# A decoder layer in fp32 on one core: the MLP's first two steps chunk by chunk, and sums and norm products on VectorE

## The chip, the core and the metric

The kernel runs on one core of one Trainium2 chip. The metric is the device time of one launch in microseconds (us). The engines are TensorE (PE in the profile; its weight loads are PEld), VectorE (DVE), ScalarE (ACT), GpSimd (POOL) and SyncE (SP), which here only issues DMAs. POOL issues DMAs too.

## The reference

One inference step of a one-layer decoder: 2048 prompt tokens, and a sample of 8 sequences with 4 new tokens each, which brings its own state. All in fp32, model width 1024.

```python
def rms_norm(x, g):
    y = x * lax.rsqrt(jnp.mean(x * x, axis=-1, keepdims=True) + EPS)
    return y * g

def decoder_layer(x, p, lp, state):          # x: (B, T, 1024)
    xn = rms_norm(x, lp['norm_mix_pre'])
    qk_raw, v_m, o_m, gates, q_a, k_a, v_a = split_projection(xn @ lp['w_in'])
    ...
    # mLSTM heads (y_m) and sliding-window attention heads (y_a)
    ...
    mix = jnp.concatenate([y_m, y_a], axis=-1) @ lp['w_out']
    x = x + rms_norm(mix, lp['norm_mix_post'])
    u = rms_norm(x, lp['norm_ffn_pre'])
    f = jnp.square(jax.nn.relu(u @ lp['w_up'])) @ lp['w_down']      # 1024 -> 4096 -> 1024
    x = x + rms_norm(f, lp['norm_ffn_post'])
    x = x + jax.nn.sigmoid(x @ lp['w_pgate']) * (p @ lp['w_pproj'])
    return x, (c_new, n_new, m_new, conv_new, k_new, v_new)
```

The change touches the MLP (`f`), the norm products around it, and the place in time of the sample's own mLSTM and attention ("decode").

## The kernel before, in words

**Blocks, chunks, groups.** The prompt is 16 blocks of 128 tokens in six chunks (3, 3, 3, 3, 2, 2 blocks). Projection, mLSTM and attention come first, up to about 700 us. The rest runs over three groups of two chunks each (`ci` 0 and 1): the product with w_out (tiles `mo`), the residual and the norms, the MLP, the gate (`pg`, `pv`). Beside the MLP's start runs what the previous stage left over, as side work. The sample's 32 rows travel with the third group, 16 of them in each chunk's columns (`HS`), so that a chunk there has 2 x 128 + 16 = 272 columns; in the first two groups it has 384.

**Products.** Every fp32 product is three fp32r matmuls: each operand is a high part (suffix h) and a low part (suffix l), and high x high, high x low and low x high are added in PSUM (`mm3`, L145 in the profile). To split a value, ACT casts it to the high part and DVE subtracts (L228 and L229: `hh`, `hl`).

**Weights.** `Ring` holds seven tiles `w` of 512 KB (high and low part of a weight block) and five raw buffers. The first use of a weight loads it raw (`wr`) on SP's queue, casts it on ACT (L249), and subtracts on POOL and DVE by turns (L250). If the plan names it again later, the tile is also stored to DRAM (`wk<-w`, L275, POOL's queue, two tiles later). Later uses load the stored pair (`w<-wk`, L282, SP's queue). The generator `plan()` lists all uses in order, and `take(n)` hands out the next n tiles; so the order of loads is the order of the plan.

**Order on PE.** PE's instructions stand in the order in which the code issues them. `Flow` keeps a model of PE's time; at each `pe.tick()` side work whose modelled time has come is put in: transposes of the next chunk's input (`tsp`), and `decode()` for the sample (`dec`; tiles with names that begin with d). `DECW` is the modelled time after which decode starts, counted from the place where it is added. `pe.drain(side)` puts in whatever is left of a side at once. The other engines' instructions are ordered by the tile framework's scheduler.

**The MLP** (`mlp`, from L1590). The 4096 hidden columns are taken in 16 steps of 256 (two tiles of 128, `ft`). Step 0 and step 1 are plain: for each chunk an up product with four weight tiles (`up`, tiles `up`, L1595), then `hidden` (L1612: relu on ACT L1617, square on ACT L1618, split L228 and L229), then the down product with four weight tiles (`down`, tiles `dn`, two for each half of the 1024 output columns), which ACT copies into `f` in step 0 and DVE adds to `f` later (L1728). In the third group chunk 1's down product is transposed (`dn200t` and so on), so that the sample's 32 rows can be taken together; for that POOL copies chunk 0's 16 hidden columns into chunk 1's tile (L1624).

Steps 2 to 15 make the up product for both chunks at once with seven products instead of eight (`up_both`). They need sums and differences of the two chunks' input blocks, made while steps 0 and 1 run: `sums()` makes seven for each half q of the columns (L1641 to L1653, tiles `ts`), each then split into `t0`, `t1`, `t2` (ACT L1658, DVE L1659). In the second and third group the half q = 1 is made on POOL, the rest on DVE. `last_sum()` (L1663 to L1675) overwrites the block that only plain steps need, so it stands behind the last plain up product.

Before the change the order was: step 0, chunk 0 up and down; drain `tsp`; chunk 1 up (with the same four tiles) and down (its four tiles loaded again); step 1: drain `dec`, add the sums; up of chunk 0, up of chunk 1, drain, last sum; down of chunk 0, down of chunk 1. These take 4 + 4 + 4 + 4 + 4 = 20 weight tiles.

**Norm products.** `finished(b, half, g, scale)` (L1433) runs when one half (512 columns) of a block's `mo` or `f` is complete: ACT squares and sums it (`j`, L1441), and the half is multiplied by the norm's gain (`gpost` behind w_out, `gffn` behind the MLP; L1443), on POOL for the first half and on DVE for the second.

Of the kernel before, what the change touches and what calls it, by code (L numbers as in the profile page):

```python
# [9 lines left out]
F32 = mybir.dt.float32  # L10
# [44 lines left out]
UENG = "d", "d", "ppp", "ppp", "", "p", "pp"  # L55
FAST = 2, 2, 2
TSP = 1.4
WBUF = 5
WIDE = 4
DECW = 5.0  # L60
DECF = 1.0
# [134 lines left out]
def hybrid_layer(ctx: ExitStack, tc: tile.TileContext, A, O):  # L196
# [195 lines left out]
    def plan():  # L392
# [36 lines left out]
        for gi in range(len(GROUPS)):  # L429
            for ci in range(2):  # L430
                for half in range(2):
                    for k in range(4):
                        yield row(w_out, k, half)
                    for k in range(4):
                        yield heads(k, half)
            for s in range(STEPS):
                if s >= FAST[gi]:
                    for i in range(7):
                        yield product(s, i)
                else:  # L440
                    for q in pairs:
                        yield two(s, q)
                for half in (0, 1, 0, 1) if s == 0 else (0, 1):
                    for k in range(s * FS, (s + 1) * FS):
                        yield row(w_down, k, half)
            for ci in range(2):
                for half in range(2):
                    embed = 0 if half == 0 and ci == 0 else 4
                    for k in range(KT):
                        if k == embed:  # L450
                            for e in range(2):
                                yield row(w_pp, e, half)
                        yield row(w_pg, k, half)
# [980 lines left out]
    def finished(b, half, g, scale):  # L1434
# [6 lines left out]
        act.activation(junk[:n, :512], v, AF.Square, scale=scale, accum_out=ms[b][:n, half : half + 1])  # L1441
        eng = (pool, dve)[half]
        eng.tensor_tensor(v, v, g[:n, half * 512 : half * 512 + 512], ALU.mult)  # L1443

# [144 lines left out]
    def mlp(gi, chunks, sample):  # L1589
# [24 lines left out]
        def hidden(s, ci, ft, t, src, hid):  # L1614
# [5 lines left out]
            split(*(y[:, :W] for y in hid[ci, ft]), t)  # L1620
            if sample and ci == 1:

                for y, z in zip(hid[0, ft], hid[1, ft]):
                    pool.tensor_copy(z[:, W : W + HS], y[:, W - HS : W].bitcast(F32))  # L1624

# [3 lines left out]
        def sums():  # L1629
# [6 lines left out]
            for q in range(2):  # L1636
                c = slice(q * n, (q + 1) * n)
                (b11, b21), (b12, b22) = [[[y[:, :, c].bitcast(F32) for y in b] for b in B[ci]] for ci in range(2)]
                t1, t2, t4 = [temp(f"ts{i}{q}", n) for i in range(3)]
                eng = pool if q and gi > 0 else dve  # L1640
                eng.tensor_tensor(t1, b12[0], b11[0], ALU.subtract)  # L1641
# [65 lines left out]
        def accumulate(s, ci, names, w, x, out, hid):  # L1707
# [9 lines left out]

            ahead = 3 if s == 0 else 1
            for i0 in range(0, len(names), ahead):
# [32 lines left out]

        X = None
        for s in range(STEPS):
            hid = {}
            fast = s >= FAST[gi]
            if not fast:
                wu = ring.take(4)
            if s == 0:

                up(s, 0, wu, hid)
                for half in range(2):
                    down(s, 0, half, down_weights(), hid)
                pe.drain(tsp)
                up(s, 1, wu, hid)
                for half in range(2):
                    down(s, 1, half, down_weights(), hid)
                continue
            if s == FAST[gi] - 1:
                pe.drain(dec)  # L1770
# [4 lines left out]
                tsp.add(sums())  # L1775
            if fast:
                up_both(s, X, hid)
            else:
                up(s, 0, wu, hid)
                up(s, 1, wu, hid)  # L1780
                if s == FAST[gi] - 1:
                    pe.drain(tsp)
                    last_sum()
            if s == STEPS - 1:
# [194 lines left out]
```

## Time and profile before

| what | value |
| --- | --- |
| runs | 2673.46, 2678.0, 2678.6 us, median 2678.0 |
| the profiled execution | 2676.5 us, of which 2674.7 are the span of the trace |
| mean granted clock of PE | 0.981 |
| DVE busy | 1481.7 us, 55% of the span |
| DMA moved | 632.23 MB, mean 236 GB/s |

In a row of the profile "L1728 DVE TENSOR_TENSOR f<-f,dn" is the instruction from line 1728 on DVE, output before the arrow, inputs behind it, with buffer numbers left out; x420 is how many there are, then the busy time of all in us and the mean of one in ns, then the engine's idle time just before them and what ended most of it. A row of waits names the waiting engine, tile and line, what it waited for, the total in us, the number of times and the longest. A row of the table by stretch gives start and end in us, the length, busy time and count of each engine, the granted clock of PE (1.00 is full speed), and DMA's share and rate. A row of the timeline gives start, duration, instruction, and in brackets the idle time before it with its releaser.

### The profile page before, as it was taken

What the parts mean: (1) busy time and instruction counts of PE and PEld (TensorE: products, weight loads), DVE (VectorE), ACT (ScalarE), POOL (GpSimd) and SP (SyncE); (2) the same over time, 40 slices, a digit from 0 to 9 for tenths busy, and PEclk for the clock granted to TensorE, in tenths of its full rate; (3) what the DMA queues carried; (4) which work ended last, traced back from release to release, by engine and by line L of the source; (5) the groups of instructions that cost most, each with busy time, mean ns of one, the idle gap of its engine ahead of it and who ended that gap; (6) DMA issues with size and microseconds to landing.
All of it is one profiled execution on the core that took longest, in us unless ns stands there. A gap on an engine that the chain in (4) does not pass through costs nothing.

```text
span 2674.7 us, 39114 instructions
## 1 busy us (share of the span) xinstructions
PE 2549.5 (95%) x14260; PEld 2212.9 (83%) x14260; DVE 1481.7 (55%) x3112; ACT 975.9 (36%) x2165; POOL 658.0 (25%) x936
## 2 busy tenths in 40 slices
PE   7899999998899999999998999999999998999998
PEld 6787878877688888888776789988888877999986
DVE  6675666664677655655735564444446345444443
ACT  5545344543455433444513432222223133222231
POOL 5311111111436666666513320000001012000010
PEclk9999999999999999999998999999999998999999
DMA  8765656666786666666987645555557885777786
GB/s 305 268 215 173 217 167 221 210 241 224 255 326 240 254 245 236 236 236 233 341 323 238 209 142 188 189 189 174 173 182 256 288 316 187 254 261 258 257 297 230
DMA packets 215186, 632.23 MB, mean 236 GB/s; under 512 B 24790, under 2 KB 58794, under 8 KB 214977
## 3 DMA queue, kind: packets, MB, share of 16 engines
q1 hardware_dynamic: 169552, 472.19, 52.0%
q0 software_dynamic: 45392, 157.50, 15.1%
q8 instruction: 113, 1.85, 0.3%
q14 instruction: 81, 0.66, 0.1%
q10 hardware_dynamic: 48, 0.03, 0.0%
HBM read 475.47 MB, written 155.25 MB: 236 GB/s over the span
## 4 chain that ended last, share of the span: by engine, by line
PE 74%; DVE 10%; DMA 6%; issue 4%; POOL 3%; ACT 2%; SPq 0%; POOLq 0%; DVEq 0%; ACTq 0%
PE dn L145 20%; PE up L145 20%; PE pg L145 5%; PE mo L145 5%; PE v L145 3%; DMA wk<-w 3%; PE qk L145 2%; DVE hl L229 2%; DMA w<-wk 2%; PE o L145 2%; PE gv L145 2%; PE qa L145 1%; PE aT L149 1%; PE aO L145 1%; PE pv L145 1%
## 5 line engine op out<-in xcount | busy, mean ns | idle before, releaser
L145 PE MATMUL dn<-w,hh 128*128 128x512 f32 x1792 | 566.6, 397 | 13.7 <-DVE f L1449 5.1
L145 PEld LDWEIGHTS dn<-w,hh 128*128 128x128 f32 x1792 | 333.2, 189 | 95.1 <-DVE f L1728 8.6
L1728 DVE TENSOR_TENSOR f<-f,dn 128x512 f32<-128x512 f32 x420 | 286.9, 687 | 222.0 <-PE dn L145 220.9
L145 PE MATMUL dn<-w,hl 128*128 128x512 f32 x896 | 355.5, 397 | 2.5 <-DVE hl L229 2.4
L1692 DVE TENSOR_TENSOR re<-up,re 128x384 f32<-128x384 f32 (+1 forms) x294 | 152.0, 517 | 326.4 <-PE up L145 326.4
L145 PEld LDWEIGHTS dn<-w,hl 128*128 128x128 f32 x896 | 169.0, 189 | 46.3 <-DVE hl L229 7.5
L1693 ACT COPY re<-up 128x384 f32<-128x384 f32 (+1 forms) x42 | 18.9, 450 | 414.8 <-PE up L145 414.8
L1617 ACT ACTIVATE re<-re 128x384 f32<-128x384 f32 (+1 forms) x168 | 83.2, 495 | 207.9 <-DVE re L1692 205.8
L229 DVE TENSOR_TENSOR hl<-re,hh 128x384 fp32r<-128x384 f32 (+1 forms) x192 | 137.7, 717 | 31.1 <-ACT hh L228 30.4
L275 POOL DMA_DIRECT2D wk<-w x242 | 134.0, 555 | 32.2 <-DVE w L250 29.2
L1443 POOL TENSOR_TENSOR f<-f,gffn 128x512 f32<-128x512 f32 x16 | 21.8, 1365 | 476.5 <-ACT j L1441 476.2
L250 POOL TENSOR_TENSOR w<-wr,w 128x512 fp32r<-128x512 f32 (+2 forms) x76 | 104.9, 1380 | 87.5 <-ACT w L249 86.6
L249 ACT CAST w<-wb 128x512 fp32r<-128x512 f32 x98 | 60.7, 621 | 173.2 <-PE dn L145 118.3
L249 ACT CAST w<-wr 128x512 fp32r<-128x512 f32 (+2 forms) x152 | 89.3, 598 | 85.6 <-PE up L145 34.3
L250 POOL TENSOR_TENSOR w<-wb,w 128x512 fp32r<-128x512 f32 x70 | 91.9, 1313 | 116.3 <-ACT w L249 115.8
L1618 ACT ACTIVATE re<-re 128x384 f32<-128x384 f32 (+1 forms) x192 | 95.1, 495 | 5.9
L228 ACT CAST hh<-re 128x384 fp32r<-128x384 f32 (+1 forms) x192 | 92.8, 483 | 6.8
L1043 ACT ACTIVATE s<-s,swt 128x257 f32<-128x257 f32 (+1 forms) x128 | 63.4, 497 | 77.5 <-DVE swt L1040 76.4
L1037 DVE CUSTOM_DVE_ANT_0 s<-aS,cst,sink 128x256 f32<-128x256 f32 (+1 forms) x128 | 57.0, 473 | 59.4 <-PE aS L145 59.2
L1624 POOL CAST hh<-hh 128x16 fp32r<-128x16 f32 x32 | 8.0, 249 | 319.0 <-ACT hh L228 319.0
L145 PE MATMUL up<-t0h,w 128*128 128x384 f32 (+1 forms) x336 | 85.1, 320 | 0.0
L145 PE MATMUL up<-t1h,w 128*128 128x384 f32 (+1 forms) x336 | 85.1, 320 | 0.0
(1537 smaller groups left out, 6530.7 us busy)
## 6 DMA issues: line engine op xcount, KB each, us to landing
w<-wk SPq DMA_DIRECT2D x692, 512.0 KB, 4.7
wk<-w POOLq DMA_DIRECT2D x238, 512.0 KB, 6.6
wr<-in_w_down_dram SPq DMA_DIRECT2D x64, 256.0 KB, 7.7
wb<-in_w_up_dram SPq DMA_DIRECT2D x28, 512.0 KB, 6.8
w<-wk SPq DMA_DIRECT2D x20, 528.0 KB, 4.4
x<-in_x_prompt_dram SPq DMA_DIRECT2D x16, 512.0 KB, 5.2
y<-yd SPq DMA_DIRECT2D x32, 256.0 KB, 7.1
xr<-in_x_prompt_dram SPq DMA_DIRECT2D x16, 512.0 KB, 6.3
```

The costliest lines, as they stand in the source:

```text
L145: ins = self.pe.matmul(out, lhsT, rhs, start=start, stop=stop)
L228: act.copy(hi, src)
L229: dve.tensor_tensor(lo, src, hi.bitcast(F32), ALU.subtract)
L249: act.copy(hi, src)
L250: (eng or weng()).tensor_tensor(lo, src, hi.bitcast(F32), ALU.subtract)
L275: here(put(self.kept[key], t.bitcast(U32)))
L1037: dve.tensor_tensor_reduce(s_[:, s, lo : 2 * P], pS[:, s, lo:], bias[:, j, lo:], 1.0 if s == 0 else 0.0625, sink[:, h : h + 1], ALU.add, A ...
L1043: act.activation(e_, e_, AF.Exp, bias=nm[:, s : s + 1], accum_out=sm[:, s : s + 1])
L1617: act.activation(t, src, AF.Relu)
L1618: act.square(t, t)
L1692: add = lambda out, a, b: dve.tensor_tensor(out, a, b, ALU.add)
L1728: dve.tensor_tensor(out(i), out(i), ps[i], ALU.add)
```

## The change

**Order.** Steps 0 and 1 go chunk by chunk: chunk 0 takes step 0 (up, down) and step 1 (up, down); then `tsp` and `dec` are drained and the sums are added; then chunk 1 takes step 0 and step 1 in the same way, `tsp` is drained and the last sum made. The plan names the weight tiles of both steps once for each chunk, 2 x (4 + 4 + 4 + 4) = 32 tiles. The down product in step 1 now keeps three PSUM tiles open as step 0 did (`ahead`).

**Decode's start.** `DECW` is 12.0 instead of 5.0.

**Norm products.** Both halves are multiplied on DVE.

**Sums.** All sums of the input blocks are made on DVE.

**The sample's columns.** Chunk 0's 16 hidden columns are kept in small tiles (`hs`) for as long as chunk 1 needs them; that is a second small copy on POOL for each of them.

```diff
@@ -53,11 +53,11 @@
 MPACE = 3.0
 GBUF = 2
 UENG = "d", "d", "ppp", "ppp", "", "p", "pp"
-FAST = 2, 2, 2
+FAST = 2
 TSP = 1.4
 WBUF = 5
 WIDE = 4
-DECW = 5.0
+DECW = 12.0
 DECF = 1.0
 UPW = 7.0, 7.0
 UPS = 2.8, 3.5
@@ -433,14 +433,14 @@
                         yield row(w_out, k, half)
                     for k in range(4):
                         yield heads(k, half)
-            for s in range(STEPS):
-                if s >= FAST[gi]:
+            for s in (*range(FAST), *range(STEPS)):
+                if s >= FAST:
                     for i in range(7):
                         yield product(s, i)
                 else:
                     for q in pairs:
                         yield two(s, q)
-                for half in (0, 1, 0, 1) if s == 0 else (0, 1):
+                for half in (0, 1):
                     for k in range(s * FS, (s + 1) * FS):
                         yield row(w_down, k, half)
             for ci in range(2):
@@ -1439,8 +1439,7 @@
         v = f[b][:n, half * 512 : half * 512 + 512]
         junk = jp.tile([P, D], BF16, tag="j", name=f"j{nm}{half}", bufs=2)
         act.activation(junk[:n, :512], v, AF.Square, scale=scale, accum_out=ms[b][:n, half : half + 1])
-        eng = (pool, dve)[half]
-        eng.tensor_tensor(v, v, g[:n, half * 512 : half * 512 + 512], ALU.mult)
+        dve.tensor_tensor(v, v, g[:n, half * 512 : half * 512 + 512], ALU.mult)
 
     def residual(b, rs, x):
         n, nm = tok(b)
@@ -1618,10 +1617,14 @@
             act.square(t, t)
             hid[ci, ft] = [hp.tile([P, UW], F32R, tag=f"h{e}", name=f"h{e}{nm}") for e in "hl"]
             split(*(y[:, :W] for y in hid[ci, ft]), t)
-            if sample and ci == 1:
-
-                for y, z in zip(hid[0, ft], hid[1, ft]):
-                    pool.tensor_copy(z[:, W : W + HS], y[:, W - HS : W].bitcast(F32))
+            if sample:
+
+                for e, y in enumerate(hid[ci, ft]):
+                    if ci == 0:
+                        t = hid["s", ft, e] = small.tile([P, HS], F32, tag="hs", name=f"hs{e}{nm}", bufs=8)
+                        pool.tensor_copy(t, y[:, W - HS : W].bitcast(F32))
+                    else:
+                        pool.tensor_copy(y[:, W : W + HS], hid["s", ft, e])
 
         def temp(nm, n):
             return ring.wide.tile([P, KT // 2, 2 * P], F32, tag="w", name=f"{nm}{G}")[:, :, :n]
@@ -1637,7 +1640,7 @@
                 c = slice(q * n, (q + 1) * n)
                 (b11, b21), (b12, b22) = [[[y[:, :, c].bitcast(F32) for y in b] for b in B[ci]] for ci in range(2)]
                 t1, t2, t4 = [temp(f"ts{i}{q}", n) for i in range(3)]
-                eng = pool if q and gi > 0 else dve
+                eng = dve
                 eng.tensor_tensor(t1, b12[0], b11[0], ALU.subtract)
                 yield TSP
                 eng.tensor_tensor(t4, b12[1], b11[1], ALU.subtract)
@@ -1715,7 +1718,7 @@
                 pe.tick()
 
 
-            ahead = 3 if s == 0 else 1
+            ahead = 3 if s < FAST else 1
             for i0 in range(0, len(names), ahead):
                 part = range(i0, min(i0 + ahead, len(names)))
                 for ft in range(FS):
@@ -1750,37 +1753,28 @@
         def down_weights():
             return [[t[:, :512] for t in w] for w in ring.take(FS)]
 
-        X = None
-        for s in range(STEPS):
-            hid = {}
-            fast = s >= FAST[gi]
-            if not fast:
-                wu = ring.take(4)
-            if s == 0:
-
-                up(s, 0, wu, hid)
-                for half in range(2):
-                    down(s, 0, half, down_weights(), hid)
+        X, hids = None, []
+
+        for ci in range(2):
+            if ci == 1:
                 pe.drain(tsp)
-                up(s, 1, wu, hid)
-                for half in range(2):
-                    down(s, 1, half, down_weights(), hid)
-                continue
-            if s == FAST[gi] - 1:
                 pe.drain(dec)
                 es_lp.close()
                 es_t = ExitStack()
                 tp = es_t.enter_context(tc.tile_pool(name="tp", bufs=1, side="right", reuse_waits="tile"))
                 ring.wide = es_t.enter_context(tc.tile_pool(name="wide", bufs=WIDE, side="right", reuse_waits="tile"))
                 tsp.add(sums())
-            if fast:
-                up_both(s, X, hid)
-            else:
-                up(s, 0, wu, hid)
-                up(s, 1, wu, hid)
-                if s == FAST[gi] - 1:
-                    pe.drain(tsp)
-                    last_sum()
+            for s in range(FAST):
+                if ci == 0:
+                    hids.append({})
+                up(s, ci, ring.take(4), hids[s])
+                for half in range(2):
+                    down(s, ci, half, down_weights(), hids[s])
+        pe.drain(tsp)
+        last_sum()
+        for s in range(FAST, STEPS):
+            hid = {}
+            up_both(s, X, hid)
             if s == STEPS - 1:
                 es_t.close()
                 open_lp()
```

Line numbers move by a few: the sums stand at L1644 to L1656, their splits at L1661 and L1662, the additions to `f` at L1731, the norm product at L1442.

**PE, third group, behind chunk 0's down product of step 0.** `dn` are down products of chunk 0; `ut150t`, `ut151t` and `ut1st` are transposes of the last block and of the sample's rows; `ut20` and `ut21` are the inputs of chunk 0 and chunk 1. Before:

```order
L145 MATMUL dn_20812<-w_20806,hh_20762 128x512 x2
L145 MATMUL dn_20812<-w_20806,hl_20763 128x512
L149 MATMUL ut150t<-ident,f_20408 128x128 x4
L149 MATMUL ut151t<-ident,f_20408 128x128 x4
L149 MATMUL ut1st<-ident,fs 128x32 x8
L145 MATMUL up_20859<-ut21h_20678,w_20666 128x272
```

After:

```order
L145 MATMUL dn_20868<-w_20862,hh_20814 128x512 x2
L145 MATMUL dn_20868<-w_20862,hl_20815 128x512
L149 MATMUL ut150t<-ident,f_20456 128x128 x4
L149 MATMUL ut151t<-ident,f_20456 128x128 x4
L145 MATMUL up_20906<-ut20h_20466,w_20898 128x272
L145 MATMUL up_20906<-ut20l_20468,w_20898 128x272
...
L149 MATMUL ut1st<-ident,fs 128x32 x8
L145 MATMUL up_20959<-ut20h_20466,w_20898 128x272
```

Before, chunk 1's up product stands right behind the transposes of its own last block; after, step 1 of chunk 0 stands there, whose input has been there since before step 0.

**PE, second group, decode's first transposes.** `mo` is the product with w_out in the second group's mix, `dph` the transposes of the sample's convolution rows (`hrow`, loaded from DRAM) and of its projection; `yt9t` to `yt11t` are transposes for chunk 1's mix. Counted from the first `mo` of this stage, 27 `mo` matmuls stand ahead of the first `dph` before, and 54 `mo` matmuls and 12 transposes after. Before:

```order
L145 MATMUL mo_14221<-w_14258,yt10h_13904 128x512 x2
L145 MATMUL mo_14221<-w_14258,yt10l_13906 128x512
L149 MATMUL dph<-ident,hrow 128x24
L149 MATMUL dph<-ident,zqk 128x32
...
L145 MATMUL mo_14221<-w_14260,yt10h_13904 128x512 x2
L145 MATMUL mo_14221<-w_14260,yt10l_13906 128x512
L149 MATMUL yt9t<-ident,y_14234 128x128 x4
```

After:

```order
L149 MATMUL yt11t<-ident,y_14264 128x128 x4
L145 MATMUL mo_14333<-w_14338,yt10h_13929 128x512 x2
L145 MATMUL mo_14333<-w_14338,yt10l_13931 128x512
...
L145 MATMUL mo_14335<-w_14338,yt10h_13929 128x512 x2
L145 MATMUL mo_14335<-w_14338,yt10l_13931 128x512
L149 MATMUL dph<-ident,hrow 128x24
L149 MATMUL dph<-ident,zqk 128x32
```

Decode's first instructions on PE move behind 27 more `mo` matmuls and behind the transposes of three more blocks.

**POOL and DVE, second group, the sums of the half q = 1.** `ts` are the sums, `ut10` and `ut11` the inputs of the two chunks. Before, on POOL:

```order
L1641 TENSOR_TENSOR ts_15762<-ut11h_15133,ut10h_14649 128x4x192
L1643 TENSOR_TENSOR ts_15764<-ut11l_15135,ut10l_14651 128x4x192
L1645 TENSOR_TENSOR ts_15762<-ts_15762,ts_15764 128x4x192
L1647 TENSOR_TENSOR ts_15763<-ut11h_15134,ts_15762 128x4x192
L1649 TENSOR_TENSOR ts_15763<-ts_15763,ut11l_15136 128x4x192
```

After, on DVE, where all fourteen now stand, from the first:

```order
L1644 TENSOR_TENSOR ts_15664<-ut11h_15157,ut10h_14624 128x4x192
L1646 TENSOR_TENSOR ts_15666<-ut11l_15159,ut10l_14626 128x4x192
L229 TENSOR_TENSOR hl_15695<-re_15691,hh_15694 128x384
L1648 TENSOR_TENSOR ts_15664<-ts_15664,ts_15666 128x4x192
L1650 TENSOR_TENSOR ts_15665<-ut11h_15158,ts_15664 128x4x192
L1662 TENSOR_TENSOR t0l_15659<-ts_15664,t0h_15658 128x4x192
L1652 TENSOR_TENSOR ts_15665<-ts_15665,ut11l_15160 128x4x192
L229 TENSOR_TENSOR hl_15730<-re_15726,hh_15729 128x384
```

POOL holds none of the sums any more; on DVE they stand among the splits (L229) of chunk 1's hidden tiles.

## The prediction

> **What bounds it now.** I read the page first: its busy times say that the matrix engine sets the time.
>
> ```profile
> PE 2549.5 (95%) x14260; PEld 2212.9 (83%) x14260; DVE 1481.7 (55%) x3112; ACT 975.9 (36%) x2165; POOL 658.0 (25%) x936
> ```
>
> PE lacks 125 us of the 2674.7 us span, and the edit removes no product. So the question is which waits of PE and which stretches at a reduced clock lie where the edit moves work. I cut the places out with a table by stretch. Its columns are length, then busy time and count for PE, weight loads, DVE, ACT, POOL; granted clock, DMA share, GB/s.
>
> ```profile
> 738.70:776.00 37.30, 37.23 (x176) 30.08 (x175) 21.91 (x45) 17.96 (x37) 14.80 (x19) 1.00 0.92 345
> 775.00:851.00 76.00, 71.96 (x364) 63.10 (x363) 64.01 (x90) 42.16 (x77) 32.63 (x33) 1.00 0.67 235
> 1404.00:1421.00 17.00, 7.97 (x34) 5.95 (x32) 6.52 (x24) 2.31 (x5) 10.75 (x22) 0.60 0.51 149
> 1506.00:1558.00 52.00, 52.00 (x286) 42.36 (x286) 25.94 (x62) 30.97 (x69) 6.71 (x9) 1.00 0.56 190
> 1558.00:1600.00 42.00, 36.94 (x174) 31.88 (x174) 36.11 (x35) 13.00 (x22) 14.41 (x7) 0.96 0.30 100
> 2197.00:2245.00 48.00, 33.05 (x183) 29.39 (x182) 32.69 (x51) 18.53 (x40) 16.47 (x15) 0.79 0.52 179
> 2205.00:2213.00 8.00, 4.15 (x12) 3.29 (x13) 4.01 (x11) 2.61 (x6) 1.89 (x4) 0.57 1.03 396
> 2222.00:2230.00 8.00, 6.63 (x30) 6.43 (x31) 7.93 (x9) 2.01 (x5) 5.05 (x3) 0.57 0.00 1
> 2236.00:2244.00 8.00, 4.17 (x18) 3.97 (x19) 5.52 (x9) 2.77 (x7) 2.27 (x2) 0.57 0.20 80
> 2245.00:2271.00 26.00, 26.00 (x185) 24.93 (x185) 8.97 (x17) 7.80 (x18) 1.33 (x4) 1.00 0.55 190
> ```
>
> Steps 0 and 1 of the first group run from 775 to 851, those of the second from 1506 to 1600, those of the third from 2197 to 2271. The loss grows from group to group. In the third, 183 matmul rows take 48.0 us and the next 185 of about the same mix take 26.0 us, so some 22 us are lost there. The second group loses 5.1 us of idle time and a little clock, the first about 4 us. At 1404 decode's start leaves PE idle for 9 of 17 us.
>
> **What the change does to each.** *First group, 775 to 851.* PE's waits there are these:
>
> ```profile
> PE dn L145 <- DVE hl L229: 1.9, 1, 1.9
> PE dn L145 <- ACT hh L228: 1.0, 1, 1.0
> PE up L145 <- DVE ut01l L237: 0.9, 1, 0.9
> ```
>
> The up product of chunk 1 no longer follows right on its norm (0.9 goes); the turn from hidden to down remains in every step (1.9 and 1.0 may stay: there are four such turns now, three before). What is new are the weights. Before, two steps took 20 tiles; now 32, which is 12 more of 512 KB in each of three groups, 36 loads and 18.9 MB in all.
>
> ```profile
> w<-wk SPq DMA_DIRECT2D x692, 512.0 KB, 4.7
> wk<-w POOLq DMA_DIRECT2D x238, 512.0 KB, 6.6
> ```
>
> Here chunk 0 meets 16 tiles for the first time, one after the other: each is loaded raw (0.26 MB), split, and stored (0.52 MB), 12.6 MB within chunk 0's two steps. Half of the 72 us that PE works between 775 and 851 is 36 us, so 350 GB/s are needed. Row 738.70 is the nearest: there 16 tiles were made at 345 GB/s with PE busy for 37.23 of 37.30 us. 12.6 MB at 345 take 36.5 us. From below, the extra loads hide wholly and the waits go: −4. From above, each of the 12 extra loads shows for 1 us: +12. I take +3, close to the row that kept PE busy. ACT's casts for the next tiles stand ahead of ACT's copies out of PSUM, and a cast waits for the store of the tile whose buffer it takes (6.6 us): that is what the upper end holds.
>
> *Decode's start.* PE comes to decode's first transposes long before their operand has landed, then runs at half clock (0.60 in row 1404.00; a pair of mo matmuls takes 1.22 us instead of 0.62):
>
> ```profile
> 1403.96 0.40 PE L145 MATMUL mo<-w,yt10l 128*128 128x512 f32 x1
> 1413.38 0.27 PE L149 MATMUL dph<-ident,hrow 24*128 24x24 f32 x1 [9.03 <-DMA hrow<-in_state_mlstm_conv_dram]
> 1414.34 1.22 PE L145 MATMUL mo<-w,yt10h 128*128 128x512 f32 x2
> ...
> PE dph L149 <- DMA hrow<-in_state_mlstm_conv_dram: 9.0, 1, 9.0
> PE dpU L145 <- DVE skm L1275: 2.4, 1, 2.4
> PE dpX L145 <- issue: 2.3, 1, 2.3
> PE dn L145 <- ACT hh L228: 2.3, 1, 2.3
> PE dn L145 <- ACT re L1617: 2.3, 1, 2.3
> ```
>
> With DECW at 12, PE's order puts 27 more mo matmuls and 12 transposes ahead of them. At 0.23 us (half a pair's start-to-start) and about 0.1 that is 6.2 + 1.2 = 7.4 us, so PE arrives at about 1411.8 for a landing at 1413.3: about 7.5 of the 9.0 go. The load itself waits for nothing that the edit moves. The half clock behind it ran for some 7 us and lost about 3.5; with a gap of 1.5 I take that as gone. Decode's later steps lie nearer to each other (dpU behind one skm buffer, dpX): between nothing and another 4 us more, I take +1. Sum −10, from −15 to −4.
>
> *Second group's steps.* Of the last two rows both waits of 2.3 us (steps' turns, while half the sums run on POOL and DVE together) have this cause:
>
> ```profile
> L1643 POOL TENSOR_TENSOR ts<-ut11l,ut10l 128x768 f32<-128x768 f32 x1 | 2.5, 2505 | 2.8 <-DVE t0l L1659 2.8
> L1651 DVE TENSOR_TENSOR ts<-ut10h,ts 128x768 f32<-128x768 f32 x1 | 2.5, 2494 | 0.0
> L1647 DVE TENSOR_TENSOR ts<-ut11h,ts 128x768 f32<-128x768 f32 x1 | 1.0, 961 | 0.0
> ```
>
> A DVE sum takes 0.96 us by itself and 2.5 beside POOL's. Now POOL has none: fourteen sums of 0.96 are 13.4 us of DVE, in the about 34 us of PE work of chunk 1's two steps. The 4.6 us of waits and the 1.7 that a clock of 0.96 over 42 us costs go. New are one or two sums queued on DVE ahead of a hidden tile's low half (0 to 1.9) and the last of decode, drained without a product beside it (about 1): net −5, from −9 to +2.
>
> *Third group's steps.* Waits there:
>
> ```profile
> PE dn L145 <- DVE f L1449: 5.1, 1, 5.1
> PE dn200t L145 <- issue: 4.1, 1, 4.1
> PE up L145 <- ACT ut21h L236: 2.3, 1, 2.3
> PE up L145 <- DVE ut21l L237: 1.4, 1, 1.4
> PE dn200t L145 <- ACT re L1617: 1.2, 1, 1.2
> ...
> 2234.16 1.70 POOL L1651 TENSOR_TENSOR ts<-ut20h,ts 128x544 f32<-128x544 f32 x1
> 2235.81 0.69 POOL L1624 CAST hl<-hl 128x16 fp32r<-128x16 f32 x1
> 2236.46 1.81 POOL L1653 TENSOR_TENSOR ts<-ut20l,ts 128x544 f32<-128x544 f32 x1
> ```
>
> The 5.1 stay: that residual waits for a load which SyncE issues behind the gain's load, and neither is moved. The 2.3 and 1.4 go, since step 1 of chunk 0 now stands between chunk 0's down product and chunk 1's up product. The 1.2 and the 4.1 come while the sample's little copies stand on POOL between sums of 1.7 us; both reasons leave POOL. That is 9.0. The clock was 0.57 in three places (rows 2205, 2222, 2236); the first follows the 5.1 and stays, the other two have 4 to 7 us of work at half rate each, say 5.5 lost together. New: sums queued ahead of the hidden tiles' splits, about 2 as above; and 32 tiles, 16.8 MB, in the about 48 us of PE work there, 350 GB/s, for which row 2205 shows 396 and row 738.70 shows 345: about 0.5 more. Net −12, from −18 (nothing new) to −4 (5 us of weight waits, one clock dip staying).
>
> *The norm's products.*
>
> ```profile
> L1443 POOL TENSOR_TENSOR f<-f,gffn 128x512 f32<-128x512 f32 x16 | 21.8, 1365 | 476.5 <-ACT j L1441 476.2
> L1443 DVE TENSOR_TENSOR f<-f,gffn 128x512 f32<-128x512 f32 x16 | 13.0, 812 | 4.2 <-ACT j L1441 4.1
> ```
>
> Thirty-two products of 1.37 us on POOL become some 0.8 on DVE. Each belongs to the first half of a block, and the second half's comes later, so it isn't last in the chain; DVE, busy for 55%, takes 26 us more in pieces between PE's matmuls. Zero, from −2 to +4.
>
> Sum: +3 − 10 − 5 − 12 + 0 = −24. Against the profiled execution's own 2676.5 that is 2652.5; the median of the runs, 2678.0, lies 1.5 above it, so **2654**.
>
> [...] Row 2222 has a clock of 0.57 with PE busy for 6.63 of its 8 us, and the only waits ahead of it are the 2.3 and 1.4: here gaps that short already cost clock. [...]
>
> **Rivals.** *The clock doesn't come back.* If the dips of row 2222 and of the second group come from something other than the short gaps, their 2.7 and 1.7 stay: −20, 2658. [...] Chance 0.07.
>
> *The stalls only move.* DVE now holds everything that POOL did, and chunk 1's hidden tiles queue behind sums at all eight places of groups two and three: 1.9 each is 15, which eats those groups' gain to −2; with decode's −10 and +3 to +5 elsewhere that leaves −8, 2670. For it: hl waits already appear among PE's. Against: DVE was free for 16 of 48 us in row 2197 with its operations stretched by POOL. Chance 0.16.
>
> *Weights become the bound (slower).* Place: chunk 0's 16 made tiles in the first group, and all 32 in the third, where down and up leave about 1.5 us a tile. It decides by the rate reached: together 29.4 MB must pass beside 80 us of PE work without loss, at 370 GB/s. If only the 235 of row 775 are reached, these take 125 us, 45 more, and the second group's 16.8 MB take 71 instead of 67, 4 more. All else at its best gives −39 (decode −15, second group −9, third −9 of waits and −5.5 of clock); so +10, 2688. The break-even is at about 250 GB/s. For it: the stores and casts wait on each other, and DMA showed 235 in just this stage. Against: that stage asked for no more, and 345 and 396 stand in the rows. Chance 0.17.
>
> *All waits go* and nothing new comes, each term at its lower end: −4 − 15 − 9 − 18 = −46, 2632. Chance 0.08.
>
> **How the numbers follow.** The forecast keeps 0.52. Its terms' spreads, added as squares (8, 6, 6, 7, 3), give about 14 us either side, 2640 to 2668. The range for 8 in 10 reaches to 2636 below (half of the last rival outside) and to 2676 above, which takes in the moved stalls and leaves out the slower rival. A measurement of this kernel can tell about 0.2%, 5.4 us, from no change. Faster by more: nearly all of 0.52, 0.07, 0.10 of the moved stalls, 0.08: 0.76. Within: 0.04 of the moved stalls, 0.03 of the slow case, 0.01: 0.08. Slower: 0.16.
>
> **What would show it.** In the changed profile: the wait for hrow near 1.5 us and the stretch behind it at full clock; no wait of PE on chunk 1's ut in the third group's steps, no 4.1 us gap there, but the 5.1 again; DVE sums of 0.96 us throughout; in the first group a DMA share near 0.9 in chunk 0's steps with PE still busy for over 90%. Wrong: PE waits on "w" of several us in steps 0 and 1 (the slower rival), or many hl waits of 1 to 2 us (moved stalls).

## The result, and the profile after

Four runs of the changed kernel took 2653.0 to 2659.81 us, median 2657.02, beside 2675.73 for the kernel before: a ratio of 0.9934, 95% interval 0.9919 to 0.9949. Six later runs of it had a median of 2651.17 and a ratio of 0.9917, 0.9901 to 0.9933. So it is faster by 19 to 23 us; 24 were forecast, from 2678.0, the median of its first three runs, to 2654. Executions of one kernel spread widely: the one before had 2666 to 2681 in all comparisons, so single stages are compared below rather than totals.

The page of the changed kernel, the line of the engines:

```profile
PE 2545.7 (96%) x14260; PEld 2211.4 (83%) x14260; DVE 1480.7 (56%) x3160; ACT 974.4 (37%) x2165; POOL 596.6 (22%) x952
```

The span fell from 2674.7 to 2655.4, PE's busy time hardly: what went is waiting. Now the stages between the same landmarks, in rows of the table by stretch (start and end, length; PE, weight loads, DVE, ACT, POOL; clock, DMA share, GB/s). Before: first group's steps 0 and 1 (to the first sum product of step 2), second group's mix (from its first `mo` to its first `up`), second group's steps, third group's steps.

```profile
775.60:855.20 79.60, 75.56 (x385) 66.78 (x385) 64.10 (x90) 43.51 (x80) 36.79 (x38) 1.00 0.65 230
1397.90:1506.50 108.60, 94.83 (x446) 72.19 (x445) 54.51 (x145) 32.66 (x74) 43.12 (x69) 0.91 0.75 237
1506.50:1603.70 97.20, 92.14 (x478) 77.54 (x477) 61.90 (x95) 44.14 (x91) 21.12 (x15) 0.98 0.46 155
2197.60:2273.80 76.20, 61.25 (x385) 56.65 (x384) 41.89 (x68) 26.38 (x59) 17.80 (x19) 0.87 0.55 188
```

After, in the same order:

```profile
773.00:863.30 90.30, 80.09 (x386) 70.18 (x385) 65.66 (x90) 42.74 (x80) 30.67 (x38) 0.92 0.77 273
1406.90:1510.60 103.70, 96.67 (x447) 72.90 (x446) 54.77 (x151) 33.22 (x74) 32.20 (x59) 0.92 0.79 245
1510.60:1601.40 90.80, 90.08 (x478) 76.58 (x477) 56.23 (x102) 44.32 (x91) 7.07 (x13) 1.00 0.70 239
2191.30:2256.40 65.10, 58.28 (x386) 53.16 (x385) 39.20 (x75) 25.93 (x59) 8.45 (x20) 0.95 0.87 319
```

The first group lost 10.7 us, its clock fell to 0.92; the other three stages gained 4.9, 6.4 and 11.1. That is 11.7 gained in all. The remaining 7.6 of the 19.3 lie in many places: 2.2 ahead of 701 us, in code that the edit doesn't touch, 4.0 between the second group's steps and the third's, and 1.9 behind the third group's steps.

PE's waits after, the longest of each place: first group (two rows), second group's mix and steps (five), third group's steps (two).

```profile
PE dn L145 <- DVE hl L229: 6.5, 3, 3.8
PE dn L145 <- ACT hh L228: 3.7, 2, 2.1
...
PE dpU L145 <- DVE skm L1275: 2.4, 2, 1.6
PE mo L145 <- DMA w<-wk: 1.8, 1, 1.8
PE dpI L145 <- DVE sW L1208: 1.5, 1, 1.5
PE dph L149 <- DMA hrow<-in_state_mlstm_conv_dram: 0.8, 1, 0.8
PE dn L145 <- ACT hh L228: 0.5, 1, 0.5
...
PE dn L145 <- ACT ju L1480: 4.5, 1, 4.5
PE dn200t L145 <- DVE hl L229: 0.6, 1, 0.6
```

As forecast, hrow's wait is nearly gone, the 5.1 of the third group stays (4.5, now put down to the operation behind that residual), and the waits for chunk 1's input and the 4.1 have gone. Not forecast: 10.2 us of waits for hidden tiles in the first group, and two new waits of 1.8 and 1.5 in the mix, where the 2.3 for `dpX` have gone.

The longest of the first group's waits, in the timelines of DVE, POOL and PE (start, duration, instruction, idle time before it):

```profile
785.45 2.39 DVE L250 TENSOR_TENSOR w<-wr,w 128x512 fp32r<-128x512 f32 x1
787.76 2.40 DVE L237 TENSOR_TENSOR ut01l<-g,ut01h 128x512 fp32r<-128x512 f32 x1
790.08 0.55 DVE L229 TENSOR_TENSOR hl<-re,hh 128x384 fp32r<-128x384 f32 x1
...
785.99 1.29 POOL L250 TENSOR_TENSOR w<-wr,w 128x512 fp32r<-128x512 f32 x1
788.32 1.27 POOL L250 TENSOR_TENSOR w<-wr,w 128x512 fp32r<-128x512 f32 x1
...
790.68 0.79 PE L145 MATMUL dn<-w,hl 128*128 128x512 f32 x1 [3.81 <-DVE hl L229]
```

PE waits for `hl`. It takes DVE 0.55 us, but stands behind two operations of 2.4 us, and each of these runs beside a subtraction of POOL for a weight tile. The same DVE operation (L237) takes 0.68 at 784.79, where POOL only issues stores. This turn from hidden to down costs PE 5.4 of the 10.2 us (1.5 for `hh` and 3.8 for `hl`). The other waits lie at two later turns, 2.7 and 2.2 us:

```profile
810.76 0.83 ACT L1661 CAST t2h<-ts 128x768 fp32r<-128x768 f32 x1 [1.57 <-DVE ts L1656]
811.50 0.52 ACT L1617 ACTIVATE re<-re 128x384 f32<-128x384 f32 x1
...
849.54 2.07 DVE L229 TENSOR_TENSOR hl<-re,hh 128x384 fp32r<-128x384 f32 x1
849.91 1.27 POOL L307 TENSOR_TENSOR wb<-wb 128x512 f32<-128x512 f32 x1
```

At the first of them ACT casts a sum, for which it waits for DVE, ahead of the hidden tile's square. At the second the split itself takes 2.07 beside a POOL operation that prepares weights for step 2; the kernel before has an `hl` wait of 1.9 in this stage too, at another turn.

### The profile page after: what moved, and what is told of

It reads as the page before. It is cut to its first block, busy times and chain, and to the rows that moved or that the text cites. A ratio compares the mean times of both kernels' runs of the same rounds, so it can differ in the third digit from the quotient of the medians.

```text
span 2655.4 us, 39328 instructions
## 1 busy us (share of the span) xinstructions
PE 2545.7 (96%) x14260; PEld 2211.4 (83%) x14260; DVE 1480.7 (56%) x3160; ACT 974.4 (37%) x2165; POOL 596.6 (22%) x952
## 4 chain that ended last, share of the span: by engine, by line
PE 74%; DVE 10%; issue 6%; DMA 5%; ACT 3%; POOL 2%; SPq 0%; DVEq 0%; POOLq 0%; ACTq 0%
PE up L145 22%; PE dn L145 21%; PE mo L145 5%; PE pg L145 4%; PE v L145 3%; PE qk L145 2%; DMA w<-wk 2%; PE qa L145 2%; PE gv L145 2%; DVE hl L229 2%; PE o L145 1%; DMA wk<-w 1%; PE aT L149 1%; PE aO L145 1%; PE pv L145 1%
## 5 line engine op out<-in xcount | busy, mean ns | idle before, releaser
L145 PE MATMUL dn<-w,hh 128*128 128x512 f32 x1792 | 567.4, 398 | 11.7 <-ACT hh L228 4.6
L1731 DVE TENSOR_TENSOR f<-f,dn 128x512 f32<-128x512 f32 x420 | 287.1, 686 | 209.7 <-PE dn L145 207.5
L229 DVE TENSOR_TENSOR hl<-re,hh 128x384 fp32r<-128x384 f32 (+1 forms) x192 | 135.3, 705 | 44.9 <-ACT hh L228 43.9
L1454 POOL TENSOR_TENSOR ms<-ms,nhalf 128x1 f32<-128x1 f32 x32 | 19.8, 629 | 587.5 <-DVE ms L1453 569.0
L249 ACT CAST w<-wb 128x512 fp32r<-128x512 f32 x98 | 60.4, 620 | 169.9 <-PE dn L145 109.2
L249 ACT CAST w<-wr 128x512 fp32r<-128x512 f32 (+2 forms) x152 | 89.0, 597 | 89.6 <-PE up L145 34.1
L145 PE MATMUL up<-t2h,w 128*128 128x384 f32 (+1 forms) x336 | 85.1, 320 | 0.0
```

What stands on the lines that cost most here:

```text
L145: ins = self.pe.matmul(out, lhsT, rhs, start=start, stop=stop)
L229: dve.tensor_tensor(lo, src, hi.bitcast(F32), ALU.subtract)
L249: act.copy(hi, src)
L1731: dve.tensor_tensor(out(i), out(i), ps[i], ALU.add)
```

## The experiments

All times are against the kernel before on the same chip. The stages are read off each profile by the same landmarks; "executions" are all runs of a kernel.

| kernel | median us | ratio, 95% interval | first group's steps | second's mix | second's steps | third's steps |
| --- | --- | --- | --- | --- | --- | --- |
| before | 2674 to 2676 | | 79.6 | 108.6 | 97.1 | 76.3 |
| changed | 2657.02 | 0.9919 to 0.9949 | 90.3 | 103.7 | 90.8 | 65.1 |
| changed, again | 2651.17 | 0.9901 to 0.9933 | 89.3 | 101.3 | 90.8 | 66.0 |
| order alone | 2679.61 | 1.0003 to 1.0022 | 89.1 | 107.3 | 99.8 | 69.8 |
| decode's start alone | 2681.67 | 1.0005 to 1.003 | 79.5 | 111.4 | 106.0 | 76.7 |
| sums alone | 2663.91 | 0.9941 to 0.9965 | 81.1 | 110.5 | 94.8 | 67.1 |
| norm products alone | 2670.13 | 0.9971 to 0.9992 | 79.9 | 106.2 | 97.0 | 77.7 |
| changed, POOL's sums back | 2667.22 | 0.9957 to 0.9983 | 90.1 | 100.2 | 98.8 | 70.9 |
| changed, start back at 5.0 | 2661.17 | 0.9936 to 0.9965 | 87.2 | 109.2 | 90.1 | 65.9 |
| changed, first group in old order | 2648.63 | 0.9888 to 0.9917 | 82.2 | 98.5 | 90.8 | 65.4 |
| changed, weights made on DVE | 2646.61 | 0.9886 to 0.9916 | 80.4 | 97.6 | 90.8 | 65.4 |
| changed, two skm buffers | 2650.17 | 0.9899 to 0.9926 | 89.6 | 95.5 | 90.8 | 65.8 |
| weights on DVE and two skm | 2648.25 | 0.9887 to 0.992 | 81.7 | 95.5 | 90.9 | 65.7 |
| all three | 2641.71 | 0.9861 to 0.9896 | 78.5 | 97.0 | 90.8 | 65.9 |

### Each part alone

**The order alone.** The edit is the diff's order, plan and small tiles, with these three lines as before:

```diff
-DECW = 12.0
+DECW = 5.0
-        dve.tensor_tensor(v, v, g[:n, half * 512 : half * 512 + 512], ALU.mult)
+        eng = (pool, dve)[half]
+        eng.tensor_tensor(v, v, g[:n, half * 512 : half * 512 + 512], ALU.mult)
-                eng = dve
+                eng = pool if q and gi > 0 else dve
```

> Before with the new order alone (steps 0 and 1 chunk by chunk, 32 tiles a group); decode's start, the norm products and the sums are as before. Theory: the order by itself loses in the first group and wins in the third. First group, from the first up of step 0 to the first sum product of step 2: 79.6 us before, about 90 here (as in the full change), since the loss there comes from the weights' low halves of chunk 0 falling between chunk 0's hidden tiles. Third group: 76.3 before, about 69 here, since the waits for chunk 1's input (2.3 and 1.4) and a clock dip go while POOL's sums stay. Second group: within 3 of 97.1. Total: between -4 and +6. Rival (the third group's gain is due to the sums and not to the order): third group stays at 74 to 77, total +8 to +13.

All as the theory had it: the first group's loss (89.1) belongs to the order, and so does some of the third group's gain (76.3 to 69.8). By itself the order is a little slower, by 1 to 6 us.

**Decode's start alone** (`DECW = 12.0`).

> Before with decode's start at 12.0 alone. Theory: PE meets hrow's landing with under 1.5 us of wait instead of 9.0, and the second group's mix, from its first mo to its first up, takes 103 to 105 us instead of 108.6, because a part is given back by decode's dpU products, which then run at half clock. Total -3 to -6. Rival (the wait only moves to other steps of decode): the mix stays at 107 to 109, total 0 within 2.

The theory fell: slower, and the mix 111.4. (The profile is of the slowest of the twelve executions, 6 us above their median, so its stages show the loss at its largest.) The wait for hrow did shrink, to 3.1, but the second group's steps took 8.9 more. Their waits, ACT's timeline at the longest, and the stretch from there on:

```profile
PE dn L145 <- ACT re L1617: 7.4, 1, 7.4
PE dn L145 <- DVE f L1728: 3.1, 1, 3.1
...
1585.75 0.83 ACT L1658 CAST t1h<-ts 128x768 fp32r<-128x768 f32 x1 [3.36 <-POOL ts L1649]
1590.30 0.83 ACT L1658 CAST t2h<-ts 128x768 fp32r<-128x768 f32 x1 [3.72 <-POOL ts L1653]
1591.04 0.48 ACT L1617 ACTIVATE re<-up 128x384 f32<-128x384 f32 x1
...
1586.00:1603.20 17.20, 8.54 (x19) 6.29 (x20) 15.93 (x18) 4.50 (x7) 4.19 (x2) 0.50 0.01 3
```

ACT's order puts two casts of sums ahead of the hidden tile's relu. Each waits over 3 us for POOL, PE idles for 7.4 us, and the clock is at half for 17 us.

**The sums alone** (`eng = dve` in `sums`).

> Before with all sums on DVE alone. Theory (DVE and POOL stretch each other's sums, and the splits of hidden tiles and the sample's copies queue behind them): the second group's steps 0 and 1 take 91 to 94 us instead of 97.1, the third group's 68 to 72 instead of 76.3; total -8 to -12. Rival (seven more sums on DVE cost as much as POOL's did; the gains in the full change come from the order): both stages within 2 of before, total 0 within 3.

The theory held: -12 in total, the third group's steps 67.1, a little better than expected; the second group's, 94.8, a little worse.

**The norm products alone** (both halves on DVE in `finished`).

> Before with the norm's products all on DVE alone. Theory: nothing waits on the first half's product, so the total is within 3 us of before; at most the wait for the last block's transposes at the end (4.1) shrinks by 1 to 2. Rival (POOL's products delay the second half and the residual, or stretch DVE): mixes and gates of all groups get shorter together by 4 us or more.

The median is 5.5 lower, the interval 2 to 8, so the theory's 3 were missed. Of the profile's 6.6, 3.9 lie ahead of 701 us, where the edit changes nothing. The mix of the second group is 2.4 shorter, but there hrow landed earlier (its wait is 6.8 instead of 9.0). The one clear place is the wait at the end, as expected at most. Before, and here:

```profile
PE xt150t L149 <- DVE xt21l L229: 4.1, 1, 4.1
```

```profile
PE xt150t L149 <- DVE xt21l L229: 2.6, 1, 2.6
```

The other profiles show a little more. Steps 2 to 15 of the second group take 446.6 to 447.4 us in all ten with both halves on DVE and 448.3 or 448.4 in the four with one on POOL; from the third group's first gate product to the end it is 79.4 to 81.3 against 82.7 to 83.5. So some 3 us go with this part. Whether the rest is the edit's or a chance of the executions stays open.

### The parts together

The four parts alone give +4, +6, -12 and -5.5, together -7 or so; the change gives -19 to -23. So at least two of them need each other.

**POOL's sums back** in the changed kernel (`eng = pool if q and gi > 0 else dve`).

> The changed kernel with the sums of the half q = 1 back on POOL in groups two and three. Theory: POOL's slow sums, with ACT's casts of them standing ahead of hidden tiles, are what made the later decode start alone slower (one wait of 7.4 for ACT in the second group's step 1). Here then: second group, from its first mo to its first sum product, 199 us or more instead of 194.5; third group's steps 68 to 71 instead of 65.1; total 7 to 15 above the changed kernel. Rival (it was decode's tail between two up products of step 1, which the new order removes): second group within 2 of 194.5, third within 2 of 65.1, total within 4 of the changed kernel.

The second group's steps take 98.8 instead of 90.8, the third's 70.9 instead of 65.1, the total 10 to 16 more. (The two stages of the second group together, 198.9, come out just under the 199 that were put down, because the mix was 3.5 shorter in this execution.) That is what POOL's sums cost in the new order. It doesn't show that they made the later start slow: the order alone, with POOL's sums and the early start, has 99.8 and 69.8 in these stages, hardly other than 98.8 and 70.9. And the mix falls from 107.3 there to 100.2 here, so the later start can pay beside POOL's sums too. (The two runs also differ in the norm products; with these alone that stage was 2.4 shorter.)

**Decode's start back at 5.0** in the changed kernel.

> The changed kernel with decode's start back at 5.0. Theory (the term of the prediction, -10 for a later start): the wait for hrow is 7 to 9 us again with some 7 to 10 us at half clock behind it; from the second group's first mo to its first sum product 201 to 206 us instead of 194.5; total 6 to 10 above the changed kernel. Rival (what the later start saves, decode's tail gives back at the end of chunk 0's steps, where it is drained): within 3 of 194.5 and within 4 us in total.

10 us above the changed kernel on the same chip, 4 above its first median. The wait and what comes with it are back in the mix, 109.2:

```profile
PE dph L149 <- DMA hrow<-in_state_mlstm_conv_dram: 8.2, 1, 8.2
PE dpU L145 <- DVE skm L1275: 2.4, 1, 2.4
PE dpX L145 <- issue: 2.3, 1, 2.3
```

The steps behind take 90.1, so the two stages give 199.2, short of the 201 expected. The later start that costs 6 us alone gains 4 to 10 in the changed kernel. The run with POOL's sums back points to the new order or the norm products as what makes the difference, rather than to the sums. That is not shown: the later start with POOL's sums gone and all else as before was not run.

### The first group's loss

**The first group in the old order**, the others in the new one; in `mlp`, too, the first group runs steps 0 and 1 as the kernel before did:

```diff
-            for s in (*range(FAST), *range(STEPS)):
+            for s in (range(STEPS) if gi == 0 else (*range(FAST), *range(STEPS))):
-                for half in (0, 1):
+                for half in ((0, 1, 0, 1) if gi == 0 and s == 0 else (0, 1)):
...
+        if gi == 0:
...
```

> The changed kernel with the old order in the first group alone (20 tiles there, both chunks in step 1 together). Theory: the first group's steps 0 and 1 fall from 90.3 back to 79 to 82 us, all else as in the changed kernel; total 2646 to 2650, 26 to 30 under before. Rival (the loss only moves: the old order delays the weights or the sums of that group): 85 or more there, total within 5 of the changed kernel.

82.2, just above what was expected, and 2648.63: the loss belongs to the order in that group, and is not moved elsewhere.

**The weights' low halves on DVE** for the tiles of steps 0 and 1, new order in all groups:

```diff
-                wsplit(h, l, raw)
+                wsplit(h, l, raw, dve if key[0] == w_down.tensor.name and key[1] < FAST * FS else None)
...
-                wsplit(h, l, raw)
+                wsplit(h, l, raw, dve if key[0] == "u" else None)
```

> The changed kernel with the low halves of the weight tiles of steps 0 and 1 made on DVE at their first use, none on POOL. Theory (the waits of PE for hl and hh in the first group come from DVE's operations that take 2.1 to 2.4 us instead of 0.55 to 0.69 while POOL makes a weight's low half): the first group's steps take 81 to 85 us instead of 90.3, with a hl wait under 1.5 at the first turn. Rival A (the density of weights: the casts on ACT and the loads and stores set it): 88 or more. Rival B (DVE gets too long a queue): 92 or more.

80.4 in the first group, just under what was expected. Its row, its waits, and DVE at the place that is quoted above for the changed kernel:

```profile
773.40:853.80 80.40, 76.55 (x386) 66.54 (x385) 62.05 (x95) 42.77 (x80) 24.00 (x32) 1.00 0.83 299
...
PE dn L145 <- DVE hl L229: 2.0, 1, 2.0
PE dn L145 <- ACT re L1616: 1.1, 1, 1.1
...
784.87 0.55 DVE L229 TENSOR_TENSOR hl<-re,hh 128x384 fp32r<-128x384 f32 x1
785.33 0.68 DVE L237 TENSOR_TENSOR ut01l<-g,ut01h 128x512 fp32r<-128x512 f32 x1
785.93 0.68 DVE L250 TENSOR_TENSOR w<-wr,w 128x512 fp32r<-128x512 f32 x1
```

All 32 tiles are still loaded, at 299 GB/s, more than in the changed kernel; DVE makes more tiles and is busy for less time (62.05 instead of 65.66), since its operations are back at 0.68, instead of 2.39 and 2.40 in the changed kernel. The waits fall from 10.2 to 3.6 (two small ones of 0.3 and 0.2 included) and the clock is 1.00. So it is POOL's making of weights beside DVE, not the weights' traffic; that POOL issues stores beside these operations (from 785.73 for 3.15 us here) doesn't stretch them. The 2.0 that stays is the wait at the last turn.

### The clock in decode's tail

**Two buffers for skm** (`bufs=2`).

> The changed kernel with two buffers for decode's skm instead of one. Theory: PE's waits for skm (0.8 and 1.6) go, and with them half or more of the 13.7 us at half clock that follow them at 1486.7; from the second group's first mo to its first up 97 to 100 us instead of 103.7. Rival (the half clock comes from decode's dpU products themselves, which use 32 of the array's rows, and not from the gaps): the half clock stays for 10 us or more and the stage takes 101 to 103.

The mix takes 95.5 at full clock, less than expected, with 1.0 us of waits for skm left. But the run with POOL's sums, with one buffer and the same two waits (0.83 and 1.56), had full clock there too. So the changed kernel was run again:

> The changed kernel once more, to see whether the 13.7 us at half clock at decode's dpU products (1486.7 in its first profile) belong to the kernel or to the one execution. In the run with POOL's sums the same products stood behind the same two waits for skm (0.83 and 1.56) at full clock. Theory (how the free-running clock falls on these products differs from one execution to the next): the length of the half-clock stretch there differs from 13.7 by 3.4 or more, and the total lies between 2650 and 2660. Rival (the kernel sets it): 13.7 again within one step of 3.4.

The stretch at half clock behind those waits was 6.8 us long instead of 13.7, two steps of 3.41 us instead of four. The 13.7 us in question, first of the changed kernel, then of its second execution, then with POOL's sums back:

```profile
1486.70:1500.40 13.70, 13.70 (x35) 9.56 (x34) 2.60 (x8) 0.59 (x1) 2.47 (x4) 0.50 0.44 122
```

```profile
1481.30:1495.00 13.70, 13.70 (x49) 9.85 (x49) 3.16 (x11) 1.76 (x3) 2.49 (x5) 0.75 0.52 146
```

```profile
1486.70:1500.40 13.70, 13.37 (x61) 10.11 (x62) 4.37 (x13) 2.26 (x5) 4.12 (x8) 1.00 0.68 208
```

The same instructions, 35, 49 or 61 rows in the same time. So part of what the skm run gained is the execution's chance. With one buffer and full clock at this place the mix takes 97.6 to 100.2 (POOL's sums back, first group in old order, weights made on DVE), with two buffers 95.5 to 97.0 in three runs. That leaves some 2 us for the second buffer, not 8.

### Together

> The changed kernel with both edits that helped alone: the low halves of steps 0 and 1's weights made on DVE, and two buffers for skm. They act in different stages, so the gains add: -10 in the first group's steps and -4 to -8 in the second group's mix; total 2638 to 2644. Rival (part of both gains was the clock's chance): 2645 to 2650.

> The same with the old order in the first group as well. Theory (order and making on DVE remove the same waits there): the first group's steps take 77 to 81 us, the total lies within 3 us of the run without the old order. Rival (their gains add): 74 or less there, total 5 or more below it.

Making on DVE with two skm buffers: 2648.25, executions from 2642.68 to 2651.73; the rival's range, so the two gains did not add. Its profile has both stages short, 81.7 and 95.5; but with DVE making alone the mix was at 97.6 already. With the old order in the first group too, 2641.71 from four runs, a ratio of 0.9879 (0.9861 to 0.9896), the lowest median here, though its interval overlaps those of the runs next to it. Its first group is 3.2 us shorter (78.5), as the theory had it; the total is 6.5 lower, outside the 3 that were expected. The rest isn't explained by a stage: of the two profiled executions the one with the old order is 1.1 slower (2644.07 and 2642.93).

## Why the prediction was right, and where not

*The sum.* -24 was forecast, -19 to -23 measured; the sign is right, and so are the mechanisms of two terms. That the size came so close is partly luck. The four stages of the sum give -11.7 in the first profile and -14.2 in the second, about half of what was forecast: two terms were mis-sized, by +8 and +5 in the first. The rest of the kernel gave 7.6 in the first profile, of which some 3 go with the norm products, which were put at nothing, and 2.2 lie ahead of everything that the edit touches.

*First group: +3 forecast, +10.7 measured (9.7 in the second execution), within the bounds (-4 to +12).* The failed step is the +3, taken from row 738.70, and the cause behind the upper end: the extra loads each showing for 1 us, and ACT's casts held up by stores. Row 738.70 is no precedent: of the 16 tiles loaded there 11 are stored pairs, and only five are made. No wait for a weight is among PE's waits in the first group. What was missed: with the sixteen first uses close together, POOL's subtractions stretch two DVE operations from 0.68 to 2.4 right ahead of a hidden tile's split, and PE waits for `hl`. DVE operations of over 1.3 us are no more frequent than before, seven in the stage in both profiles; it is their place that is new. The row for this (0.96 alone, 2.5 beside POOL) stood in the prediction, used for the sums only. The run with DVE making the weights shows it for the largest wait. That a sum's cast stands ahead of a hidden tile at the middle turn (2.7 us) is read off the trace alone.

*Decode's start: -10 forecast, -4.9 and -7.3 measured in two executions.* The idle part came as worked out: 9.0 fell to 0.8 and 1.0. The +1 for new waits was near, too: 1.8 for a weight, 1.5 for decode's sW and 0.5 came, 2.3 for `dpX` went. The failed step is the half clock taken as gone. Behind hrow it is gone (1.00 from 1410.0 to 1435.5, with the wait for hrow at 1421), but it came back, for 3.41 us behind the 1.8 for a weight and for 13.7 behind the waits for skm: the stage has 17.1 us of it in the first profile and 10.2 in the second, beside 20.5 before. In the runs in which the clock held there the mix took 95.5 to 100.2, which is -8 to -13. That the late start needs another part of the change to pay was not seen at all; alone, it was slower.

*Second group's steps: -5 forecast, -6.4; third group's: -12 forecast, -11.1.* Both right, with the mechanisms named: without POOL's sums DVE's take 0.95 (0.72 in the third group, whose tiles are smaller), the sample's copies come in time, and step 1 of chunk 0 covers chunk 1's norm. How the parts meet the sum didn't say. In the third group they overlap: the sums alone give -9.2, the order alone -6.5. In the second group's steps they need each other: the sums alone give -2.3, the order alone costs 2.7, and together (decode's start at 5.0) it is -7.0.

*Norm products: 0 forecast, from -2 to +4; -5.5 alone, of which some 3 go with the edit* and 1.5 are located, in the wait at the end. The failed step is that the first half's product was taken to be never last in the chain: with it on DVE the wait at the end is 2.6 instead of 4.1.

*The rivals.* Weights as the bound: refuted, the third group's steps ran with 319 GB/s and the first group's, with weights on DVE, with 299; the 235 of before was demand, not a limit. Moved stalls: not where the rival put them; PE waits 0.8 us for `hl` in the third group's steps and not at all in the second's. The waits for `hl` came in the first group, whose sums had been on DVE before. The clock not coming back: in the third group it rose from 0.87 to 0.95 and in the second group's steps to 1.00.

## What to carry to other kernels

When one engine slows another, look for every place where they meet, not only the one the change mentions: here POOL beside DVE cost much where weights are split (0.68 us became 2.4). Look, too, at what stands in an engine's order behind an operation that waits: here two casts on ACT waited 3.36 and 3.72 us for POOL's sums ahead of a relu, and PE idled for 7.4 us. Try parts together as well as alone, and take one out again before saying which of them need each other. Where executions of one kernel differ by 10 us, compare stages between landmarks, and run a profile twice before explaining a stretch at half clock (13.7 us of it here, then 6.8).

## What was not expected of the hardware

The same products behind the same two waits of 0.83 and 1.56 us ran at half clock for 13.7 us, 6.8 us, and not at all, in three executions (rows above); within the 13.7 us PE showed as busy throughout. So short gaps can cost clock, but need not. The traces show what differs. In the profiles of before and after, each change of the clock lies on a grid of steps of 3.41 us, within 3 ns (1486.72 less 786.98, two falls in the changed kernel's profile, is 205 of them). The grid lies elsewhere in the two executions, by 1.1 us if counted from the start of the span. Here are the steps around the 1.56 us, in the changed kernel and with weights on DVE:

```profile
1483.30:1486.72 3.42, 1.86 (x9) 1.38 (x9) 2.93 (x6) 0.72 (x2) 0.82 (x2) 1.00 0.86 284
1486.72:1490.13 3.41, 3.41 (x10) 2.31 (x9) 1.13 (x3) 0.00 (x0) 0.22 (x1) 0.50 0.09 35
...
1473.93:1477.34 3.41, 2.98 (x14) 1.84 (x12) 3.28 (x7) 1.38 (x4) 1.36 (x3) 1.00 0.62 177
1477.34:1480.76 3.42, 2.29 (x11) 1.64 (x11) 2.29 (x5) 0.72 (x2) 0.18 (x1) 1.00 0.78 240
```

In the changed kernel the whole 1.56 us lie in one step (3.42 less 1.86), and the fall comes at its end. With weights on DVE an edge of the grid lies between the two parts of the idle time, 0.43 and 1.13 us, and both steps are at full clock. Counted over the profiles of before and after, behind 650 us, the clock fell after all 20 steps at full clock in which PE idled for 1.92 us or more. Of seven with 1.51 to 1.83 us it fell after three (1.56, 1.65 and 1.83) and held after four (the longest 1.71). Of the other 1111 it fell after one, with 1.37 us, in the kernel before. That one holds products of the sample (`ut0st`, at 2185.32), as the step of the 1.56 us does (`dpU`, 32*128 in the profile's rows). Whether these narrow products have a part in it is not shown.
